# Turning between two sets of PSUM banks in an MLP's second product, and starting its first product early, in a two-layer hybrid network

## The chip, the cores and the metric

The kernel runs on one core of a Trainium2 chip. The metric is device time in microseconds (us) for one execution of the whole program, less is better. Names of engines: PE multiplies matrices (TensorE) and PEld is its loading of weights, DVE is VectorE, ACT is ScalarE, POOL is GpSimd, and SP issues the DMAs.

## The reference

A two-layer network on 1024 tokens with a model width of 1024, all in fp32. Layer 0 mixes tokens by attention in a sliding window, layer 1 by a gated recurrence (HGRN2), and each is followed by the same MLP, which is where the change lies:

```python
def sqrelu_mlp(h, w_up, w_down):
    return jnp.square(jax.nn.relu(h @ w_up)) @ w_down

for layer in range(DEPTH):                      # 2
    h = rmsnorm(x, mix_norm[layer])
    y = attention(h) if layer % 2 == 0 else hgrn2(h)
    x = x + y
    h = rmsnorm(x, mlp_norm[layer])
    x = x + sqrelu_mlp(h, w_up[layer], w_down[layer])   # w_up 1024x4096, w_down 4096x1024
return rmsnorm(x, final_norm)
```

## The kernel before, in words

**Precision.** Every fp32 operand is split into two numbers of a shorter format, a high part `hi` and the rest `lo`. A product is three matmuls (`mm3`): hi·hi, hi·lo, lo·hi. A split (`split`, `weight_split`) is one cast, on ACT or DVE, and one subtraction on DVE. Weights that are split as they come lie in small rings of buffers, `wr` (raw), `wh` and `wl` (5 of each); activations and everything that lives longer lie in the 60 buffers named `a`; `t` (18) and `m` (7) are for short use.

**Strassen.** Both products of the MLP are done by one level of Strassen's scheme (Winograd's form), with seven products, numbered 1 to 7, in place of eight. Sums of blocks of the weights and of the activations are made on DVE before, and sums of the results after.

**The first product** (`pair`, 16 calls with m = 0 to 15) makes rows m and m+16 of the hidden layer, each 128 wide, for both halves of the 512+512 tokens. Products 1 and 2 need the first half of the tokens only (`self.b[1]`, `self.b[2]`, made by `begin`), the others need sums with the second half (`finish`). Pairs 0 and 1 do all seven at full size (`leaves` empty); from pair 2 on, products 2 and 4 go one Strassen level deeper and are put together for two pairs at a time. The squared ReLU of each result is written to DRAM (`self.hid`).

**The second product** (`down`) has 16 steps p over the hidden layer, and the results of all steps are summed up in PSUM: four banks `main` (tag `q`) and four banks `side` (tag `p`), one bank for each 128 output columns of one half of the output. A step of one product is 12 matmuls of 512 columns, three into each of four banks. A *pass* (`run_pass`) does all 16 steps of one product, so 192 matmuls; operands are prepared up to two steps ahead (`operands`), by loads from DRAM, one or two sums, and two splits. Products 1, 6, 7 and 4 accumulate in `main`, which goes on from one to the next, and what stands in it after a product is copied out by ACT before the next product is added; products 5, 2 and 3 use `side`. The first pass does 1 and 5 step by step in turn. `T[p]` and `S[p]` are running sums of activations and of weights, kept from pass to pass in `a` buffers. Before, the passes are:

(1,5), 6, 7, 4, 2, 3

so that after (1,5) three passes in a row write `main`, and then two in a row write `side`. The last 4 steps of pass 3 (8 in layer 1) are held back and done at the end, bank by bank, under the beginning of what follows: in layer 0 the recurrence's normalisation and first products (`hgrn_first`, `hgrn`), in layer 1 the final norm (`final`).

**The order of the work.** The code only records operations. A planner (`Schedule.order`) then goes through time with a cost for each operation, gives buffers in the order of the program, and on each engine takes the operation with the lowest rank (its place in the program, less a lead for loads and splits of weights) among those that are ready. So each engine has a fixed list, worked off strictly in that order on the chip: an instruction that waits holds up all behind it. An operation with two possible engines (a cast) goes to where the planner sees it done first. All instructions carry line 334 in the profile, that of the call that issues them; so groups are told apart by names of buffers.

Of the kernel before, what the change touches and what calls it, by code (L numbers as in the profile page):

```python
# [14 lines left out]
ALU = mybir.AluOpType  # L15
# [3 lines left out]
T = 1024  # L19
# [3 lines left out]
TH = T // NH  # L23
# [112 lines left out]
LEAD = 100  # L136
WARM = 8
EVACUATE = 100
HK = KT // 2
# [140 lines left out]
class Net:  # L280
# [38 lines left out]
    def a(self, dt=F32, shape=(P, TH)):  # L319
        return self.tile("a", BUFS["a"], shape, dt)  # L320
# [251 lines left out]
        self.weigh(0)  # L572

    def mlp_second(self):
        x = self.finish(2 + self.layer, keep=True)
        self.weigh(1)
        return x
# [72 lines left out]
    def inner_products(self, leaf, w, x, sums, steps):  # L650
# [6 lines left out]
        for step in steps:  # L657
# [7 lines left out]
                self.tt("DVE", z, z, ps, ALU.add, 2 * P)  # L665
            yield

    def pair(self, m, x, leaves=()):

        up = self.io["up"][self.layer]
        first, second, half = up[m], up[m + MT // 2], MT // 2
        inner = []
        for leaf, now in leaves.items() if leaves else ():
            if now and leaf == 2:
                inner.append((2, up[m - 1][:, TH:], None))
            elif now:
                k = m - 1 if m == half - 1 else m - 2  # L680
                inner.append((4, up[k + half][:, TH:], up[k + 1 + half][:, TH:]))
        w = self.strassen_weights(first, second, tuple(leaves) if leaves else (), inner)

        def read(ps):
            z = self.t()
            self.copy(z, ps)
            return z

        parts = []

        def between():
            for z in parts:
                next(z, None)

        main, side = self.psum("q"), self.psum("q")
        self.product(main, w[1], x[1], True)
        u1 = read(main)
        if not leaves:
            own = self.psum()
            self.product(own, w[2], x[2], True)  # L700
            self.tt("DVE", u1, own, u1, ALU.add)
            self.square_relu(m, 0, u1, False)
        else:
            self.sums[2].append((m, u1))
            for leaf, now in leaves.items():
                if now and (leaf == 2 or m < half - 1):
                    sums = [z for _, z in self.sums[leaf][-2:]] if leaf == 2 else [z for _, z in self.sums[4][-2:]]
                    parts.append(self.inner_products(leaf, w, now, sums, ((1, 2), (6, 5), (7, 3), (4,))))
        between()
        self.product(side, w[5], x[5], True)  # L710
        p5 = read(side)
        between()
        self.product(main, w[6], x[6], False)
        u2 = read(main)
        self.product(side, w[3], x[3], False)
        between()
        self.tt("DVE", u2, side, u2, ALU.add)
        self.square_relu(m, 1, u2, False)
        last = leaves and leaves.get(4) and m == half - 1
        if last:  # L720
            u3 = self.t()
            z = self.inner_products(4, w, leaves[4], [self.sums[4][-1][1], u3], ((1, 2), (6,), (5, 7), (3, 4)))
            next(z)
        self.product(main, w[7], x[7], False)
        if last:
            next(z)
            self.copy(u3, main)
        else:
            u3 = read(main)
        between()  # L730
        self.tt("any", p5, p5, u3, ALU.add)
        self.square_relu(m + half, 1, p5, False)
        if not leaves:
            self.product(main, w[4], x[4], False)
            self.square_relu(m + half, 0, main, True)
            return
        if last:
            run(z)
            self.sums[4].append((m + half, u3))
            for n, u in self.sums[2][-2:] + self.sums[4][-2:]:  # L740
                self.square_relu(n, 0, u, False)
            return
        if leaves.get(2):
            for n, u in self.sums[2][-2:]:
                self.square_relu(n, 0, u, False)
        if leaves.get(4):
            for n, u in self.sums[4][-2:]:
                self.square_relu(n, 0, u, False)
        self.sums[4].append((m + half, u3))
# [26 lines left out]
    def operands(self, name, p, T, S, held=False):  # L776

        a = lambda i, k: self.raw(self.io["down"][self.layer, k, p, :, i])
        h = lambda i, hf: self.hidden(i, hf, p)

        def sum_of(tile, x, y, alu=ALU.subtract):
            self.tt("any", tile, x, y, alu)
            return tile

        if name == 1:
            self.corner = a(0, 0), h(0, 0)
            w, x = self.corner
        elif name == 5:
            first, q00 = self.corner
            T[p] = x = sum_of(self.a(), h(0, 1), q00)  # L790
            w = sum_of(self.t(tag="m"), a(1, 0), a(1, 1), ALU.add)
        elif name == 6:
            T[p] = x = sum_of(T[p], h(1, 1), T[p])
            w = S[p]
        elif name == 7:
            x = sum_of(self.t(), h(1, 1), h(0, 1))
            w = sum_of(self.t(tag="m"), a(0, 0), a(1, 0))
        elif name == 4:
            x = sum_of(T[p], h(1, 0), T[p])
            w = a(1, 1)  # L800
        elif name == 2:
            w, x = a(0, 1), h(1, 0)
        else:
            x = h(1, 1)
            w = sum_of(S[p], a(0, 1), S[p])
        got = self.split(w) if held else self.weight_split(w), self.split(x)
        if name == 5:
            S[p] = sum_of(self.a(), w, first)
        return got

    def down(self, cut):
# [4 lines left out]
        n, ahead = MT // 2, 2  # L816
# [4 lines left out]
        def products(names, ps, ws, start, stop, tokens=slice(0, TH), ms=range(HK)):  # L821
            for p in ps:
                for name in names:
                    (wh, wl), (xh, xl) = ws[name, p]
                    for m in ms:
                        out = (main if name in (1, 6, 7, 4) else side)[m][:, tokens]
                        c = slice(m * P, m * P + P)
                        more = {"skip_group_check": True} if name in (6, 7, 4) or not start else {}
                        first = p == 0 and not more
                        self.mm3(out, (wh[:, c], wl[:, c]), (xh[:, tokens], xl[:, tokens]), first, p == stop,  # L830
                                 tokens.stop - tokens.start, **more)

        def run_pass(names, held=0):
            ws, todo = {}, list(range(n))
            for p in range(n):
                while todo and todo[0] <= p + ahead or (todo and todo[0] >= n - held and p >= n - held - 1):
                    q = todo.pop(0)
                    for name in names:
                        ws[name, q] = self.operands(name, q, T, S, q >= n - held)
                if p < n - held:  # L840
                    products(names, [p], ws, True, n - held - 1)
            return ws

        def scaled_sum(hf, out, z, tokens=slice(0, TH)):
# [7 lines left out]
        def residual(m, hf):  # L852
            z = self.a()
            self.dma(z, self.x[m][hf], 4 * P * TH)
            return z

        run_pass((1, 5))
        for m in range(HK):
            y[0, 0, m], y[1, 1, m] = self.a(), self.a()
            self.copy(y[0, 0, m], main[m])  # L860
        for m in range(HK):
            self.copy(y[1, 1, m], side[m])
        run_pass((6,))
        for m in range(HK):
            u = y[0, 1, m] = self.a()
            self.copy(u, main[m])
        for m in range(HK):
            self.tt("DVE", y[0, 1, m], y[0, 1, m], y[1, 1, m], ALU.add)
        run_pass((7,))
# [5 lines left out]
        for i in range(2):  # L875
            for m in range(HK):
                z = residual(m + (1 - i) * HK, 1)
                scaled_sum(1, z, y[1 - i, 1, m])
                self.x[m + (1 - i) * HK][1] = z
        run_pass((4,))  # L880
        for m in range(HK):
            z = residual(m + HK, 0)
            scaled_sum(0, z, main[m])
            self.x[m + HK][0] = z
        run_pass((2,))
        parts = [self.t() for _ in range(HK)]
        for m in range(HK):
# [1 line left out]
        for m in range(HK):  # L889
            self.tt("DVE", y[0, 0, m], parts[m], y[0, 0, m], ALU.add)  # L890
            z = residual(m, 0)
            scaled_sum(0, z, y[0, 0, m])
            self.x[m][0] = z
        if not cut:
            held = 4
            ws = run_pass((3,), held)
            yield 0, slice(0, TH)
            for m in range(HK):
                products((3,), range(n - held, n), ws, False, n - 1, ms=[m])
                scaled_sum(1, self.x[m][1], side[m])  # L900
            yield 1, slice(0, TH)
            return
        held = n // 2
# [637 lines left out]
```

## Time and profile before

| | |
|---|---|
| three runs | 2151.45, 2154.43, 2158.83 us |
| the profiled execution | 2151.11 us, of which the profile's span is 2149.3 us |
| granted PE clock, mean | 0.996 |
| DVE busy | 1866.9 us (87%) |
| ACT busy | 993.3 us (46%) |
| moved by DMA | 333.91 MB, 155 GB/s on average |
| layer 0: first products / second products | 344 to 636 us / 636 to 938 us |
| layer 1: first products / second products | 1504 to 1817 us / 1817 to 2110 us |

Times within the execution count from the start of the span. In the rows of the profile, a group such as `q<-a,wh` is an instruction that writes a `q` bank from an `a` buffer and a `wh` buffer. `[2.30 <-ACT t]` at the end of a row of the timeline is the idle time of the engine before it, and the engine and buffer that ended it. A matmul's row is longer than its share of PE, since matmuls overlap; the distance of two starts tells the pace. Rows by stretch give, for each engine, busy time and the number of instructions, then the granted PE clock (1.00 is full), the share of the DMA engines, and GB/s.

### The profile page before, as it was taken

Reading aid. Unit: us, or ns where it says so; the run is one execution under the profiler, and the core shown is the slowest. Engines: PE = TensorE matmul, PEld = TensorE weight load, DVE = VectorE, ACT = ScalarE, POOL = GpSimd, SP = SyncE. Lnnn points to the kernel's source line nnn. Section 1 sums busy time; section 2 is a strip of 40 time slices with the busy share of each in tenths; the row PEclk is TensorE's granted clock in tenths of the full one; section 3 lists DMA queues with packets and bytes.
Section 4 is the critical chain, followed back from the end, with each engine's and each line's share of the span. In section 5 each row is a group of like instructions: output and inputs, shape, how many; then the busy total and the mean of one; then the engine's idle time right before and its main releaser. Section 6 shows DMA issues by size and latency. Waiting matters only on the chain.

```text
span 2149.3 us, 33980 instructions
## 1 busy us (share of the span) xinstructions
PE 2114.5 (98%) x11968; PEld 1734.0 (81%) x11968; DVE 1866.9 (87%) x3822; ACT 993.3 (46%) x2031; POOL 61.7 (3%) x121
## 2 busy tenths in 40 slices
PE   9999999999999999999999999999999999999998
PEld 7778777888888887877788888788788888888787
DVE  8889899888899988899888888878988889899886
ACT  5567777444454234465333333343644445423444
POOL 4020000000000000000100000000000000000000
PEclk9999999999999999999999999999999999999999
DMA  6212275443468876731111111547444446897652
GB/s 214 77 50 83 80 245 167 131 134 124 137 197 293 299 248 219 255 111 55 59 60 55 60 55 60 189 155 227 165 133 133 128 132 202 282 301 244 200 177 79
DMA packets 183787, 333.91 MB, mean 155 GB/s; under 512 B 20672, under 2 KB 22720, under 8 KB 183616
## 3 DMA queue, kind: packets, MB, share of 16 engines
q1 hardware_dynamic: 183616, 331.74, 47.3%
q8 instruction: 94, 1.54, 0.3%
q14 instruction: 77, 0.63, 0.1%
HBM read 265.60 MB, written 66.06 MB: 154 GB/s over the span
## 4 chain that ended last, share of the span: by engine, by line
PE 54%; issue 36%; DVE 5%; ACT 3%; DMA 1%; SPq 0%; POOL 0%; POOLq 0%; ACTq 0%; DVEq 0%
PE p L334 29%; PE q L334 25%; DVE a L334 2%; DVE t L334 2%; ACT a L334 1%; ACT t L334 1%; DVE wl L334 1%; DVE m L334 1%; DMA t<-d 0%; ACT wh L334 0%; DVE wh L334 0%; DMA wr<-in_up 0%; DVE sm L334 0%; DMA a<-in_x 0%; DMA d<-t 0%
## 5 line engine op out<-in xcount | busy, mean ns | idle before, releaser
L334 PE MATMUL p<-a,wh 128*128 128x512 f32 (+1 forms) x2616 | 775.0, 378 | 5.8 <-ACT wh L334 4.0
L334 PE MATMUL q<-a,wh 128*128 128x512 f32 x2336 | 734.9, 396 | 6.8 <-ACT t L334 5.0
L334 PEld LDWEIGHTS p<-a,wh 128*128 128x128 f32 x2616 | 469.3, 188 | 96.5 <-ACT wh L334 5.0
L334 PEld LDWEIGHTS q<-a,wh 128*128 128x128 f32 x2336 | 432.1, 189 | 102.6 <-ACT t L334 7.5
L334 PE MATMUL p<-a,wl 128*128 128x512 f32 (+1 forms) x1308 | 488.5, 374 | 1.8 <-DVE wl L334 1.7
L334 PE MATMUL q<-a,wl 128*128 128x512 f32 x1168 | 460.9, 395 | 0.3 <-DVE wl L334 0.3
L334 PEld LDWEIGHTS p<-a,wl 128*128 128x128 f32 x1308 | 246.3, 188 | 46.9 <-DVE wl L334 2.7
L334 PEld LDWEIGHTS q<-a,wl 128*128 128x128 f32 x1168 | 220.1, 188 | 52.7 <-DVE wl L334 0.8
L334 DVE TENSOR_TENSOR wl<-wr,wh 128x512 fp32r<-128x512 f32 x352 | 241.2, 687 | 15.6 <-ACT wh L334 5.3
L334 ACT ACTIVATE t<-t 128x512 f32<-128x512 f32 x238 | 148.1, 631 | 169.8 <-DVE t L334 163.5
L334 DVE TENSOR_TENSOR wl<-m,wh 128x512 fp32r<-128x512 f32 x312 | 212.5, 687 | 5.1 <-ACT wh L334 0.4
L334 DVE TENSOR_TENSOR a<-t,a 128x512 fp32r<-128x512 f32 (+2 forms) x304 | 199.1, 677 | 3.4 <-DMA t<-d 2.9
L334 ACT COPY t<-q 128x512 f32<-128x512 f32 (+2 forms) x201 | 111.1, 559 | 193.0 <-PE q L334 171.7
L334 ACT CAST a<-t 128x512 fp32r<-128x512 f32 (+1 forms) x203 | 121.5, 611 | 144.1 <-PE q L334 73.9
L334 ACT CAST wh<-wr 128x512 fp32r<-128x512 f32 x180 | 111.1, 620 | 162.8 <-PE p L334 93.0
L334 DVE TENSOR_TENSOR t<-t,t 128x512 f32<-128x512 f32 (+3 forms) x299 | 173.6, 599 | 12.2 <-DMA t<-d 6.2
L334 ACT CAST wh<-m 128x512 fp32r<-128x512 f32 x200 | 123.5, 622 | 128.6 <-PE p L334 66.1
L334 DVE CAST wh<-wr 128x512 fp32r<-128x512 f32 x172 | 73.5, 428 | 118.2 <-PE q L334 78.5
L334 DVE TENSOR_TENSOR m<-wr,wr 128x512 f32<-128x512 f32 (+1 forms) x188 | 119.3, 647 | 18.8 <-DMA wr<-in_down 16.1
L334 PE MATMUL p<-wh,a 128*128 128x512 f32 x384 | 126.0, 399 | 0.5 <-ACT a L334 0.4
L334 PEld LDWEIGHTS q<-t,t 128*64 128x64 f32 (+1 forms) x2160 | 98.0, 144 | 25.0 <-issue 10.9
L334 PE MATMUL q<-t,t 128*64 128x32 f32 (+2 forms) x2160 | 111.5, 230 | 0.0
(125 smaller groups left out, 2323.7 us busy)
## 6 DMA issues: line engine op xcount, KB each, us to landing
t<-d SPq DMA_DIRECT2D x312, 256.0 KB, 4.7
wr<-in_down SPq DMA_DIRECT2D x256, 256.0 KB, 4.1
d<-t SPq DMA_DIRECT2D x188, 256.0 KB, 3.1
wr<-in_up SPq DMA_DIRECT2D x170, 256.0 KB, 3.1
wr<-in_win SPq DMA_DIRECT2D x68, 256.0 KB, 2.8
a<-d SPq DMA_DIRECT2D x60, 256.0 KB, 4.4
wr<-in_wqkv SPq DMA_DIRECT2D x48, 256.0 KB, 2.9
d<-a SPq DMA_DIRECT2D x48, 256.0 KB, 3.4
```

Of the source, the lines that this page charges most:

```text
L334: fn(*[place(a) for a in args], **{k: place(v) for k, v in kw.items()})
```

## The change

Two things are done, in both layers.

**Passes in turn.** The passes become (1,5), 6, 7, 2, 4, 3. The last step of product 5 (p = 15) is taken out of the first pass (`kept`): its operands are split into `a` buffers, and its 12 matmuls into `side` stand after pass 6. `side` is copied out after that and no more after (1,5). With 2 ahead of 4, pass 2 makes the weight sum of pass 3, `S[p] = a01 - S[p]`, from the block that it has loaded for itself, and pass 3 loads and sums no weights any more (16 loads less in each layer). `T[p]`, which pass 4 uses last, lives through pass 2.

**Products 1 and 2 of pairs 0 and 1 first.** A new function `pair_first` is called for m = 0 and 1 at the start of `mlp_second`, ahead of `finish`: it loads and splits the two blocks of weights, does products 1 and 2 on the first half of the tokens, adds them and writes the squared ReLU; the `q` bank with product 1 is handed on to `pair`, which goes on with 5. `pair` still loads the two blocks for its sums of weights, so each block comes twice (4 more loads in each layer).

In all, the list of SP has 24 rows less; the numbers of matmuls, of sums and of splits stay the same.

```diff
     def mlp_second(self):
+        self.first = [self.pair_first(m) for m in range(2)]
         x = self.finish(2 + self.layer, keep=True)
...
+    def pair_first(self, m):
+        self.s.lead = LEAD
+        up = self.io["up"][self.layer, m]
+        w = [self.weight_split(self.raw(up[:, c : c + TH])) for c in (0, TH)]
+        self.s.lead = 0
+        main, own, u1 = self.psum("q"), self.psum(), self.t()
+        self.product(main, w[0], self.b[1], True)
+        self.copy(u1, main)
+        self.product(own, w[1], self.b[2], True)
+        self.tt("DVE", u1, own, u1, ALU.add)
+        self.square_relu(m, 0, u1, False)
+        return main
...
-        w = self.strassen_weights(first, second, tuple(leaves) if leaves else (), inner)
+        w = self.strassen_weights(first, second, tuple(leaves) if leaves else (1, 2), inner)
...
-        main, side = self.psum("q"), self.psum("q")
-        self.product(main, w[1], x[1], True)
-        u1 = read(main)
-        if not leaves:
-            own = self.psum()
-            self.product(own, w[2], x[2], True)
-            self.tt("DVE", u1, own, u1, ALU.add)
-            self.square_relu(m, 0, u1, False)
-        else:
+        main, side = self.psum("q") if leaves else self.first[m], self.psum("q")
+        if leaves:
+            self.product(main, w[1], x[1], True)
+            u1 = read(main)
...
         elif name == 2:
             w, x = a(0, 1), h(1, 0)
+            S[p] = sum_of(S[p], w, S[p])
         else:
-            x = h(1, 1)
-            w = sum_of(S[p], a(0, 1), S[p])
+            w, x = S[p], h(1, 1)
...
-        def run_pass(names, held=0):
+        def run_pass(names, held=0, kept=()):
...
-                        ws[name, q] = self.operands(name, q, T, S, q >= n - held)
+                        ws[name, q] = self.operands(name, q, T, S, q >= n - held or (name, q) in kept)
                 if p < n - held:
-                    products(names, [p], ws, True, n - held - 1)
+                    products([name for name in names if (name, p) not in kept], [p], ws, True, n - held - 1)
...
-        run_pass((1, 5))
+        ws = run_pass((1, 5), kept=[(5, n - 1)])
         for m in range(HK):
-            y[0, 0, m], y[1, 1, m] = self.a(), self.a()
+            y[0, 0, m] = self.a()
             self.copy(y[0, 0, m], main[m])
-        for m in range(HK):
-            self.copy(y[1, 1, m], side[m])
         run_pass((6,))
+        products((5,), [n - 1], ws, True, n - 1)
...
+        for m in range(HK):
+            y[1, 1, m] = self.a()
+            self.copy(y[1, 1, m], side[m])
...
-        run_pass((4,))
-        for m in range(HK):
-            z = residual(m + HK, 0)
-            scaled_sum(0, z, main[m])
-            self.x[m + HK][0] = z
         run_pass((2,))
...
+        run_pass((4,))
+        for m in range(HK):
+            z = residual(m + HK, 0)
+            scaled_sum(0, z, main[m])
+            self.x[m + HK][0] = z
```

Three places of the engines' lists are shown, each before and after. The numbers behind a buffer's name tell one use of it from another.

First, PE in layer 0 at the end of pass 7, before. The banks `q1694` to `q1697` are `main`:

```order
L334 MATMUL q1697_7375<-a2208_9057,wh2206_9106 128x512
L334 MATMUL q1697_7375<-a2209_9067,wh2206_9106 128x512
L334 MATMUL q1697_7375<-a2208_9057,wl2207_9112 128x512
L334 MATMUL q1694_7326<-a2234_9136,wh2232_9132 128x512
L334 MATMUL q1694_7326<-a2235_9177,wh2232_9132 128x512
L334 MATMUL q1694_7326<-a2234_9136,wl2233_9139 128x512
```

and the same place after, where `q1698` to `q1701` are `main` and `p1702` to `p1705` are `side`:

```order
L334 MATMUL q1701_7383<-a2212_9036,wh2210_9083 128x512
L334 MATMUL q1701_7383<-a2213_9044,wh2210_9083 128x512
L334 MATMUL q1701_7383<-a2212_9036,wl2211_9089 128x512
L334 MATMUL p1702_7392<-a2238_9113,wh2236_9107 128x512
L334 MATMUL p1702_7392<-a2239_9142,wh2236_9107 128x512
L334 MATMUL p1702_7392<-a2238_9113,wl2237_9120 128x512
```

Behind pass 7 stood pass 4, in the same four banks; now pass 2 stands there, in the other four.

Second, ACT in layer 1 after the end of the recurrence's output product, before. `q3846` holds product 1 of pair 0, `q3847` its product 5, `wh3866` is the weight of pair 1's product 1; `a3793` to `a3801` are operands of product 4 that `finish` makes:

```order
L334 CAST wh3866_16618<-wr3858_16392 128x512
L334 CAST a3793_16623<-t3792_16484 128x512
L334 CAST a3797_16629<-t3796_16494 128x512
L334 CAST a3801_16635<-t3800_16505 128x512
L334 CAST wh3844_16641<-wr3827_16358 128x512
L334 COPY t3848_16645<-q3846_16521 128x512
L334 COPY t3851_16647<-q3847_16582 128x512
```

and after, where `q3738` and `q3748` hold product 1 of pairs 0 and 1:

```order
L334 ACTIVATE t3777_16520<-a3731_16511,c01_91 128x512
L334 COPY t3740_16529<-q3738_16492 128x512
L334 ACTIVATE t3812_16535<-a3661_16123 128x512
L334 ACTIVATE t3813_16542<-a3671_16169 128x512
L334 CAST a3778_16547<-t3777_16520 128x512
L334 CAST wh3842_16555<-m3837_16504 128x512
```

The copy of product 1 stood behind the casts of the operands of product 4 and now stands ahead of them, among the first instructions after the last row of `x`.

Third, ACT in layer 0 in pass 3, before. `wh2480` is the weight of step 6, `wh2486` to `wh2504` those of steps 7 to 10; the rows with `t` on the left or right belong to the recurrence's beginning:

```order
L334 CAST wh2492_10309<-a1845_7746 128x512
L334 CAST a2555_10313<-t2554_10028 128x512
L334 CAST a2559_10319<-t2558_10050 128x512
L334 CAST a2563_10326<-t2562_10071 128x512
L334 ACTIVATE t2576_10332<-a2330_9421 128x512
L334 CAST wh2486_10338<-a1829_7696 128x512
L334 CAST wh2498_10342<-a1861_7797 128x512
L334 CAST wh2504_10346<-a1877_7862 128x512
L334 CAST a2567_10348<-t2566_10107 128x512
L334 ACTIVATE t2577_10352<-a2332_9431 128x512
L334 CAST wh2480_10356<-a1813_7631 128x512
```

and after, where `wh2477` is the weight of step 6, `wh2482` that of step 7 and `wh2487` that of step 8:

```order
L334 CAST wh2482_10272<-a1833_7704 128x512
L334 ACTIVATE t2565_10276<-a2444_9884 128x512
L334 CAST a2543_10283<-t2542_10173 128x512
L334 CAST wh2477_10289<-a1817_7639 128x512
L334 CAST a2547_10295<-t2546_10182 128x512
L334 CAST wh2487_10301<-a1849_7754 128x512
```

The weight of step 6 stood behind those of the four steps that follow it, and now stands behind that of step 7 alone.

## The prediction

> **What bounds the kernel now.** I read the page's first part, then who waited for whom on PE, then the stretches around those waits in the timeline.
>
> ```profile
> span 2149.3 us, 33980 instructions
> PE 2114.5 (98%) x11968; PEld 1734.0 (81%) x11968; DVE 1866.9 (87%) x3822; ACT 993.3 (46%) x2031; POOL 61.7 (3%) x121
> PE q L334 <- ACT t L334: 6.9, 6, 2.3
> PE p L334 <- ACT wh L334: 4.0, 1, 4.0
> PE q L334 <- ACT wh L334: 1.7, 2, 1.5
> ```
>
> PE is busy for 98% of the span, and the change takes no matmul away. So what can be won is only where PE waits, or runs slowly: the last three rows say that it waited 6.9 us, in 6 waits, for results of ACT in `t`, once 4.0 us for a weight in `wh`, and 1.7 us for other such weights.
>
> ```profile
> 725.40:769.90 44.50, 44.50 (x193) 35.93 (x193) 40.01 (x72) 11.37 (x20) 0.00 (x0) 1.00 0.69 226
> 926.23:929.64 3.41, 3.41 (x9) 2.76 (x9) 3.41 (x11) 2.25 (x4) 0.00 (x0) 0.50 0.00 0
> 1516.73:1520.14 3.41, 3.41 (x8) 2.74 (x9) 3.41 (x6) 2.59 (x5) 0.00 (x0) 0.50 0.23 79
> 1998.01:2001.42 3.41, 3.41 (x8) 2.73 (x9) 3.41 (x7) 3.06 (x6) 0.00 (x0) 0.50 0.61 174
> ```
>
> The first row is pass 6 of layer 0, undisturbed: 192 matmuls in 44.5 us at clock 1.00, 0.232 us each. The other three are stretches at half the clock: 8 or 9 matmuls in 3.41 us, where 8 take 1.86 us and 9 take 2.09 us, so 1.55, 1.55 and 1.32 us lost in each. Each begins where a wait of PE ends, so a wait there costs itself and the half clock behind it.
>
> **The change part by part.** *Pass 7 to the next pass.* In layer 1, PE and ACT at the end of pass 7, and what DVE waited for in pass 7; the last row is PE's wait at the same place in layer 0:
>
> ```profile
> 1995.31 0.40 PE L334 MATMUL q<-a,wl 128*128 128x512 f32 x1
> 1996.85 0.62 ACT L334 CAST a<-a 128x512 fp32r<-128x512 f32 x1 [0.86 <-DVE a L334]
> 1997.38 1.55 ACT L334 COPY t<-q 128x512 f32<-128x512 f32 x3
> 1998.01 1.22 PE L334 MATMUL q<-a,wh 128*128 128x512 f32 x2 [2.30 <-ACT t L334]
> ...
> DVE a L334 <- DMA a<-d: 1.6, 2, 1.4
> ...
> PE q L334 <- ACT t L334: 0.8, 1, 0.8
> ```
>
> PE has done pass 7 at 1995.3 and needs `main` copied out before pass 4 writes it. ACT comes to these copies at 1997.4 only, since the cast ahead of them in its list waits for DVE, and DVE had waited 1.6 us for rows of `x` that come back from DRAM. With pass 2 behind pass 7, PE writes `side`, and the same late copies are wanted 44.5 us later. Gain: 2.30 + 1.55 = 3.85 us in layer 1, 0.82 us in layer 0. What could be late in its place is an operand of pass 2: in the new lists the steps of pass 2 after the first four have their last operand at least 6 DVE instructions ahead of PE's turn. At 0.60 us each (five sums start 1506.98 to 1509.99, below) that is 3.6 us, over the 1.6 us; cost 0.
>
> *The beginning of layer 1's MLP.* PE, ACT and DVE:
>
> ```profile
> 1503.93 0.39 PE L334 MATMUL p<-a,wl 128*128 128x512 f32 x1
> 1512.26 0.40 PE L334 MATMUL q<-a,wl 128*128 128x512 f32 x1
> 1514.12 0.72 PE L334 MATMUL q<-a,wh 128*128 128x512 f32 x2 [1.47 <-ACT wh L334]
> 1516.68 1.21 PE L334 MATMUL q<-a,wh 128*128 128x512 f32 x2 [1.84 <-ACT t L334]
> 1516.05 1.06 ACT L334 COPY t<-q 128x512 f32<-128x512 f32 x2
> 1506.98 3.09 DVE L334 TENSOR_TENSOR t<-t,t 128x512 f32<-128x512 f32 x5
> 1509.99 3.09 DVE L334 TENSOR_TENSOR a<-t,a 128x512 fp32r<-128x512 f32 x5
> ```
>
> The recurrence's output product ends on PE at 1503.9, and then products 1, 2 and 5 of pair 0 are all there is: 36 matmuls, 8.35 us, up to 1512.3. Then PE waits for the next pair's weight (1.47 us), and product 6 waits 1.84 us for the copy of product 1 out of its bank, which stood behind the casts of product 4's operands on ACT. Lost: 1.47 + 1.84 + 1.55 = 4.86 us. Now 60 matmuls stand there (products 1 and 2 of both pairs, then 5), 13.9 us, and the copy is early. Product 6's last operand is the 15th DVE instruction from the read of the output product's last bank on: 15 x 0.60 = 9.0 us and about 1 us until DVE starts, so some 10 us against 13.9. The added work: 4 loads of 256 KB, in a stretch with DMA to spare (the row 1516.73 has a share of 0.23), and pair 1's splits, copy, addition and squared ReLU, which only come earlier. DVE does them within those 15; what they push back are the operands of products 7 and 4, needed 19 and 22 us after 1503.9. I take 0.5 us as left, between 0 (the room of 3.9 us holds) and the 1.84 us of the wait that was there. In layer 0 there is no such row of any size between 344 and 367 us; I take 0.
>
> *Pass 3 and the recurrence's beginning, layer 0.*
>
> ```profile
> 919.00:925.20 6.20, 2.24 (x10) 1.50 (x8) 6.20 (x11) 6.20 (x12) 0.13 (x1) 1.00 0.15 42
> 924.61 0.60 ACT L334 CAST wh<-a 128x512 fp32r<-128x512 f32 x1
> 925.26 0.96 PE L334 MATMUL p<-a,wh 128*128 128x512 f32 x3 [4.02 <-ACT wh L334]
> ...
> 769.90:815.00 45.10, 44.53 (x193) 35.78 (x191) 41.59 (x72) 15.77 (x29) 0.00 (x0) 1.00 0.86 290
> 815.00:860.00 45.00, 44.76 (x193) 36.27 (x194) 36.71 (x63) 17.75 (x32) 0.00 (x0) 1.00 0.67 208
> 860.00:904.60 44.60, 44.60 (x194) 36.13 (x193) 35.86 (x63) 16.05 (x28) 0.00 (x0) 1.00 0.78 250
> 904.60:938.00 33.40, 29.38 (x120) 23.42 (x119) 33.40 (x83) 26.42 (x49) 0.36 (x2) 0.95 0.45 151
> ```
>
> Here nobody waits but PE: DVE and ACT are busy for all of 919.0 to 925.2 (6.20 of 6.20), and DVE for all of 904.6 to 938.0. PE waits 4.02 us for step 6's weight, cast last of its neighbours, and runs at half clock after it: 4.02 + 1.32 = 5.34 us. The change takes 16 weight sums out of pass 3 (9.6 us of DVE at 0.60), and four additions from what precedes it: pass 2's results were copied and added before scaling, pass 4's are scaled straight from PSUM. So DVE has up to 12 us less here, over the 5.34, and the new list has step 6's weight split 5 matmul groups of three before PE's turn. The sums go into pass 2. Its DVE work is then what pass 4 had (a sum and two subtractions a step, and the 20 instructions that finish passes 5 and 7): the 36.7 us of row 815 against 44.6 us of PE. Pass 4, without those 20 but with 8 scalings and 4 additions of pass 2's results, comes to 36.71 - 8 x 0.60 = 31.9 us. Both are below row 769.9's 41.59, under which PE ran without a wait until its end. I take 0.5 us of the 5.34 as left, between 0 and the whole.
>
> *The edge from (1,5) to 6.* Before, product 5's last step (12 matmuls, 2.8 us) lay between the last write of `main` by 1 and the first by 6. Now 6 follows at once. Layer 1, where DMA is nearest to its limit:
>
> ```profile
> 1817.00:1906.00 89.00, 88.61 (x388) 71.76 (x387) 80.06 (x136) 39.83 (x71) 0.00 (x0) 1.00 0.88 288
> ...
> DVE m L334 <- DMA wr<-in_down: 8.2, 9, 1.9
> ...
> 1900.92 0.62 ACT L334 CAST a<-a 128x512 fp32r<-128x512 f32 x1 [2.16 <-PE p L334]
> 1901.86 1.97 ACT L334 COPY a<-q 128x512 f32<-128x512 f32 x3 [0.31 <-PE q L334]
> 1905.37 0.69 DVE L334 TENSOR_TENSOR wl<-a,wh 128x512 fp32r<-128x512 f32 x1
> 1906.51 0.63 PE L334 MATMUL q<-a,wh 128*128 128x512 f32 x2
> 1906.98 0.39 PE L334 MATMUL q<-a,wl 128*128 128x512 f32 x1
> ```
>
> The copies start 0.3 us after PE has written the first bank, and ACT is idle before them, so the first bank is free at about 1902.5, 1.2 us ahead of its next use even without 5 between (1906.5 - 2.8 = 1903.7). The operands are nearer: DVE waited 8.2 us for weights in this pass, and pass 6's first low part ends at 1906.06, 0.92 us before its matmul at 1906.98. In the new lists pass 6's operands move up by as many DVE instructions as PE comes earlier, less one, so 0.92 - 0.60 = 0.3 us is left. I take 0.5 us lost in layer 1 for it. Bounds: a gain is excluded, since PE does not wait there now; above, DVE may be late by the whole 2.8 us, then half clock: 4.35 us. It is nearest to the lower end, by the 0.3. After pass 6, product 5's step covers the copies of `main`; there was no wait to take away.
>
> *Sum.* 3.85 + 0.82 + 4.86 + 5.34 = 14.87 us, less 0.5 + 0.5 + 0.5, is 13.4 us. The profiled execution took 2151.11 us and would take 2137.7. The median of the runs, 2154.43, is 3.3 us higher; I leave that distance and predict 2141 us.
>
> **The rivals.** *The edge fails.* Pass 6 finds its operands 2.8 us late, at half clock after: 4.35 us in place of the 0.5 in layer 1, and in layer 0 too if DMA waits are as long there. Gain 9.5 or 5.2 us, 2145 to 2149 us. For it: the reserve of 0.3 us. Against: DVE's list moves with PE's.
>
> *DVE only moves the wait.* Sums moved into pass 2 make its operands late, or pass 3 keeps its wait. It gives back the 5.34: 2146 us. For it: DVE busy all of 904.6 to 938. Against: rows 815 and 860, with 8 us of DVE idle in each.
>
> *Slower.* The first pass's DMA waits on DVE (8.2 us in 9 waits) come through to PE once the 2.8 us at its end no longer fill DVE's backlog. From the point where the reserve is below zero, each wait is PE's: 8.2 us, and six half clocks of 1.4 us, 16.6 us a layer. In both layers: 2141 + 33 = 2174 us; in one it would be about no change or a little slower (2157). Against: under those waits PE was busy for 88.61 of the 89.00 us of this pass (its row stands ahead of the waits).
>
> *Half clocks are not of the waits.* Two of the three follow waits of 2.30 us and of 1.47 + 1.84 us. The Trainium skill (TensorE: Matmul & The Clock Gate, section "Why this matters for your kernels") says the clock drops after PE idles for more than about 3 us. If these two stay when the waits go, the gain is 13.4 - 3.1 = 10.3 us, 2144 us. The rows speak against this rule: a half clock begins within 0.1 us of the end of both waits.
>
> *Turning between banks costs clock.* Passes on two sets of banks in turn could make PE idle for a moment at each change; with a half clock of 1.55 us at four more changes in each layer, 12.4 us, the time would be 2153 us. The same page of the Trainium skill ("A second HAM failure mode: psum-queue depth-cycling") reports a kernel that lost its clock by cycling through banks. Against: (1,5) turns between the sets at every step already, and the rows 1901 to 1907 show full pace.
>
> **How the numbers follow.** Chances: forecast 0.70; edge 0.11; DVE 0.08; slower 0.04; clock not of the waits 0.05; banks 0.02. 0.3% (6.5 us) is about what a measurement of this kernel can tell from no change, so faster is below 2148: the forecast, DVE, the clock and two thirds of the edge, 0.88 with some taken off for what is unknown. Around no change: the rest of the edge, banks, part of slower, 0.08; slower 0.04. The range: below, nothing left or lost (14.87) from the profiled 2151.1, and some 3 us more where the runs' own spread (2151.45 to 2158.83) held such waits: 2133. Above, the edge in both layers, 2149, with 2 us of spread: 2151.
>
> **What would show it.** Right: no wait of PE for `t` behind pass 7, in either layer; none over 1 us in 1500 to 1525 or in pass 3 of layer 0; no half clock between the first matmuls and the end but a short one; DVE less than full in pass 3. Wrong: PE waiting for `wl` at the start of pass 6, or a new wait in pass 2.

## The result, and the profile after

The changed kernel took 2134.97 us (median of 6 runs, 2134.27 to 2137.78) against 2153.54 us before (6 runs, 2148.07 to 2158.83). The ratio is 0.9919, 95% interval 0.9907 to 0.9931, which is 17.4 us less (14.9 to 20.0); the medians differ by 18.6 us. Gains against the kernel before are worked out from ratios in this way below. The forecast was 2141 us and a gain of 13.4 us, in a range of 2133 to 2151. The profiled execution took 2136.34 us.

From the page's first part and from who waited for whom on PE, after:

```profile
span 2134.6 us, 33918 instructions
PE 2108.3 (99%) x11968; PEld 1732.8 (81%) x11968; DVE 1866.6 (87%) x3828; ACT 992.3 (46%) x2026; POOL 59.8 (3%) x121
PE q L334 <- ACT t L334: 3.0, 4, 1.3
PE q L334 <- ACT wh L334: 0.2, 1, 0.2
```

PE's waits for `t` fell from 6.9 to 3.0 us, those of `q` for `wh` from 1.7 to 0.2, and the row for `p` and `wh` (4.0 us) is gone. DVE's and ACT's busy times are the same within 1 us: the work did not shrink, PE only waits less. By stretch (columns as before: busy time and instructions of PE, PEld, DVE, ACT, POOL, then the clock), after:

```profile
815.50:817.50 2.00, 2.00 (x10) 1.64 (x9) 2.00 (x4) 1.89 (x5) 0.00 (x0) 1.00 0.25 61
905.11:938.00 32.89, 32.89 (x144) 26.69 (x143) 29.97 (x77) 19.87 (x36) 0.00 (x0) 1.00 0.45 153
1501.00:1525.00 24.00, 22.99 (x101) 18.09 (x99) 24.00 (x41) 18.45 (x34) 0.00 (x0) 1.00 0.67 217
1982.00:1986.00 4.00, 4.00 (x19) 3.26 (x18) 3.23 (x7) 3.34 (x7) 0.00 (x0) 1.00 0.53 173
```

The first and last row hold the edges from pass 7 to pass 2 (816.2 and 1984.95 us): PE is busy throughout. The second is pass 3 of layer 0: 144 matmuls in 32.9 us, where 120 took 33.4 before. The third is the beginning of layer 1's MLP, the only one of the four places with a wait left, and the clock is 1.00 in all four. What is left there, in the timeline of PE and then of ACT, after:

```profile
1520.26 0.40 PE L334 MATMUL q<-a,wl 128*128 128x512 f32 x1
1520.63 0.73 PE L334 MATMUL q<-a,wh 128*128 128x512 f32 x2
1522.37 0.74 PE L334 MATMUL q<-a,wh 128*128 128x512 f32 x2 [1.01 <-ACT t L334]
...
1521.22 0.62 ACT L334 CAST wh<-m 128x512 fp32r<-128x512 f32 x1 [0.64 <-DVE m L334]
1521.74 0.58 ACT L334 COPY t<-q 128x512 f32<-128x512 f32 x1
```

This is product 4 of pair 0, which waits for the copy of product 7 out of its bank: three matmuls begin in 2.11 us, where 0.70 would do. The copy stands behind a cast that had waited 0.64 us for DVE.

Where the time went, summed over the starts of all matmuls of PE: the distance of two starts beyond the usual one of that kind of matmul (0.232 us for 512 columns) is time lost.

| place | lost before, us | lost after, us |
|---|---|---|
| start of the program (to 45 us) | 4.4 | 7.2 |
| layer 0: turn from first to second products | 1.6 | 1.4 |
| layer 0: behind pass 7 | 1.1 | 0 |
| layer 0: pass 3 | 5.8 | 0 |
| layer 0: between pass 3 and the recurrence's loop | 2.3 | 1.8 |
| layer 1: beginning of the MLP | 5.4 | 1.5 |
| layer 1: turn from first to second products | 1.7 | 1.2 |
| layer 1: behind pass 7 | 4.1 | 0 |

Without the first row that is 16.1 us less, with it 13.3 us; the two spans differ by 14.7 us, and the rest is spread over many small places. The first row is not the change's: it lies ahead of every changed instruction, and in the twelve other profiles below this stretch lost between 4.8 and 6.6 us, whichever the kernel.

### The profile page after: what moved, and what is told of

The parts are those of the page before. It is cut to its first block, busy times and chain, and to the rows that moved or that the text cites. A ratio compares the mean times of both kernels' runs of the same rounds, so it can differ in the third digit from the quotient of the medians.

```text
span 2134.6 us, 33918 instructions
## 1 busy us (share of the span) xinstructions
PE 2108.3 (99%) x11968; PEld 1732.8 (81%) x11968; DVE 1866.6 (87%) x3828; ACT 992.3 (46%) x2026; POOL 59.8 (3%) x121
## 4 chain that ended last, share of the span: by engine, by line
PE 86%; DVE 8%; issue 2%; DMA 2%; ACT 1%; POOL 0%; SPq 0%; POOLq 0%; DVEq 0%; ACTq 0%
PE q L334 44%; PE p L334 41%; DVE t L334 3%; DVE a L334 2%; DVE wl L334 1%; DVE m L334 1%; ACT a L334 1%; DMA wr<-in_up 0%; DVE wh L334 0%; DMA t<-d 0%; DMA wr<-in_win 0%; DMA a<-in_x 0%; ACT t L334 0%; DVE sm L334 0%; DMA c<-in_par 0%
## 5 line engine op out<-in xcount | busy, mean ns | idle before, releaser
L334 ACT CAST wh<-wr 128x512 fp32r<-128x512 f32 x191 | 117.8, 619 | 162.6 <-PE p L334 96.2
L334 DVE TENSOR_TENSOR t<-t,t 128x512 f32<-128x512 f32 (+4 forms) x299 | 173.4, 598 | 12.3 <-DMA t<-d 7.3
L334 ACT CAST wh<-m 128x512 fp32r<-128x512 f32 x187 | 115.4, 622 | 115.7 <-PE p L334 61.2
L334 DVE CAST wh<-wr 128x512 fp32r<-128x512 f32 x161 | 68.8, 427 | 100.2 <-PE q L334 70.6
L334 DVE TENSOR_TENSOR m<-wr,wr 128x512 f32<-128x512 f32 (+1 forms) x188 | 119.3, 645 | 17.4 <-DMA wr<-in_down 14.4
```

Source lines behind the costliest of these rows:

```text
L334: fn(*[place(a) for a in args], **{k: place(v) for k, v in kw.items()})
```

## The experiments

Each kernel ran in five rounds beside the kernel before on the same chip; ratios are to before, with their intervals. The kernels of the first group shared one chip, those of the second (rows_later, early_half, act_only, four_later) another, the last four a third. Before took 2150.39, 2149.89 and 2148.51 us there.

**The two halves apart.** `order_only` is the changed kernel without `pair_first`, `first_only` the kernel before with it.

```diff
 order_only, against after
-        self.first = [self.pair_first(m) for m in range(2)]
 first_only, against before
+        self.first = [self.pair_first(m) for m in range(2)]
```

> The new order of the passes with the last step of product 5 behind pass 6 and the weight sums in pass 2, but products 1 and 2 of pairs 0 and 1 as before. Theory A (each part took away the waits that stood at its own place, and they add up): the wait for `t` behind pass 7 and the wait for a weight in pass 3 of layer 0 are gone, the two waits at the beginning of layer 1's MLP (1.5 and 1.8 us) and the half clock behind them are back: about 12 to 14 us faster than before, ratio 0.994. Theory B (the early products matter beyond their place, since they shift the lists of all engines behind them): other waits come back too, less than 8 us faster.

> Products 1 and 2 of pairs 0 and 1 early, the passes as before. Theory A: only the beginning of the MLP changes, 4 to 5 us faster (two waits of 1.5 and 1.8 us and 1.5 us by half clock go, a wait of 1.0 us behind product 7 comes), ratio 0.998; behind pass 7 of layer 1 PE waits 1.5 to 2.5 us for `t` with half clock after it, and 4 us for a weight in pass 3 of layer 0. Theory B: more than 8 us faster.

`order_only` took 2139.09 us, ratio 0.9952 (0.9940 to 0.9964), 10.3 us less; `first_only` 2145.00 us, 0.9974 (0.9960 to 0.9988), 5.6 us less. Together 0.74%, against 0.73% (after_again, below) and 0.81% of both: the halves add up, as theory A has it, though `order_only` falls short of the 12 to 14 us that were expected. In `order_only`'s profile the two waits at the beginning of layer 1's MLP are back (1.44 and 1.83 us, with a half clock behind them), and there is none behind pass 7 nor in pass 3. In `first_only`'s those are there, in the timeline of PE:

```profile
818.68 0.74 PE L334 MATMUL q<-a,wh 128*128 128x512 f32 x2 [1.80 <-ACT t L334]
929.72 1.22 PE L334 MATMUL p<-a,wh 128*128 128x512 f32 x2 [3.44 <-ACT wh L334]
1997.37 0.92 PE L334 MATMUL q<-a,wh 128*128 128x512 f32 x2 [2.87 <-ACT t L334]
```

**Which part of the order.** `swap_only` exchanges passes 4 and 2 and nothing else; `sums_only` moves the weight sums and nothing else.

```diff
 swap_only, against before: the lines from run_pass((4,)) to self.x[m + HK][0] = z
 stand behind those of run_pass((2,))
 sums_only, against before
         elif name == 2:
             w, x = a(0, 1), h(1, 0)
+            S[p] = sum_of(S[p], w, S[p])
         else:
-            x = h(1, 1)
-            w = sum_of(S[p], a(0, 1), S[p])
+            w, x = S[p], h(1, 1)
```

> From the kernel before, only passes 4 and 2 change places; the weight sums stay in pass 3, with their loads, and product 5 stays whole in the first pass. Theory A, as predicted (pass 3's wait comes of the 16 weight sums that DVE does there): the wait behind pass 7 goes in both layers (0.8 + 3.9 us), the wait of about 4 us for a weight in pass 3 of layer 0 stays with its half clock: about 5 us faster. Theory C (pass 3's wait comes of what stands ahead of it, four copies on ACT and four additions on DVE of pass 2's results that the list must place in pass 3's first steps; behind pass 4 there are none): pass 3's wait goes too, about 10 to 11 us faster. In the new list step 6's weight no longer stands right ahead of PE's turn, which speaks for C.

> From the kernel before, only the weight sums S = a01 - S move from pass 3 into pass 2 (16 loads and 16 sums less in pass 3, no load more in pass 2); order of the passes as before. Theory A (DVE's load in pass 3): pass 3's wait of 4.0 us and its half clock go, 5 us faster; the wait behind pass 7 of layer 1 stays at 1.5 to 2.5 us. Theory C (what stands ahead of pass 3): its wait stays at 2 to 4 us and the time within 2 us of before.

`swap_only` took 2140.09 us, 0.9954 (0.9942 to 0.9966), as much as the whole of `order_only`. `sums_only` took 2151.06 us, 1.0005 (0.9995 to 1.0014): no change. Pass 3 of layer 0 by stretch, in `swap_only` and then in `sums_only`, with PE's wait there in the latter:

```profile
905.98:939.00 33.02, 33.02 (x144) 26.85 (x143) 31.77 (x80) 22.48 (x40) 0.36 (x2) 1.00 0.51 172
```

```profile
909.50:942.00 32.50, 30.11 (x124) 23.99 (x123) 31.36 (x80) 26.11 (x48) 0.36 (x2) 0.95 0.35 121
928.45 0.90 PE L334 MATMUL p<-a,wh 128*128 128x512 f32 x2 [2.39 <-ACT wh L334]
```

So the 16 weight sums in pass 3, on which the prediction built its second largest term, are not what made its wait. One row could have told it: DVE's groups in the kernel before, from the beginning of pass 3 to the end of the wait (904.6 to 926 us), have the weight sums as `a<-wr,a`:

```profile
L334 DVE TENSOR_TENSOR a<-wr,a 128x512 f32<-128x512 f32 x2 | 1.4, 681 | 0.0
```

Two of the sums stood there, 1.4 us. The others had been done ahead.

**What makes pass 3 wait.** Two explanations were left: the work that pass 2's results bring into pass 3 (theory C), or the place of one cast in ACT's list (theory P). `early_half` takes the work away, `act_only` changes the list at the same work.

```diff
 early_half, against before
+        for m in range(HK):
+            z = residual(m, 0)
+            scaled_sum(0, z, y[0, 0, m])
+            self.x[m][0] = z
         run_pass((2,))
-        parts = [self.t() for _ in range(HK)]
...
+        for m in range(HK):
+            scaled_sum(0, self.x[m][0], side[m])
 act_only, against before
-    def weight_split(self, z):
+    def weight_split(self, z, engines=("ACT", "DVE")):
...
-        got = self.split(w) if held else self.weight_split(w), self.split(x)
+        got = self.split(w) if held else self.weight_split(w, ("ACT",) if name == 3 else ("ACT", "DVE")), self.split(x)
```

> From the kernel before, the half of `y[0, 0]` that is known before pass 2 is scaled and added to `x` ahead of pass 2, so that behind pass 2 its banks are scaled straight from PSUM, as pass 4's are: no copies on ACT, no four additions on DVE behind pass 2, eight instructions of DVE more ahead of it. Theory C (work that pass 2's results bring into the first steps of pass 3 makes its weight late): the wait for a weight in pass 3 of layer 0 (4.0, 3.4 and 2.4 us in the three profiles with pass 2 ahead of pass 3) goes, 4 to 5 us faster. Theory P (the wait is where the order of the lists puts one step's cast behind those of the steps after it, which in this list is the weight of step 5 in place of step 6): a wait of over 1.5 us stays, one step earlier, and the time is within 3 us of before.

> From the kernel before, the casts of pass 3's weights that are split as they come may go on ACT alone, not on DVE. Work and order of the passes are those of before, but in ACT's list these casts now stand in the order of their steps, each 12 or more ACT instructions ahead of PE's turn. Theory P: the wait for a weight in pass 3 of layer 0 goes with its half clock, 4 to 5.5 us faster; the wait behind pass 7 stays. Theory C: with the same work the wait stays, at another step or of another buffer, and the time is that of before.

`early_half` took 2149.00 us, 0.9996 (0.9984 to 1.0007). The wait stayed, one step earlier, where its list has the cast of step 5 last:

```profile
921.98 1.19 PE L334 MATMUL p<-a,wh 128*128 128x512 f32 x4 [1.85 <-ACT wh L334]
```

`act_only` has no wait in pass 3, with the work and the order of passes of before: in both traces all 17 casts into `wh` between 890 and 945 us are on ACT and none on DVE, and their order is what the edit changes. Theory P holds: the wait is where the planner's list puts one step's cast behind those of the steps after it. But the 4 to 5.5 us that were expected did not come: 2147.82 us, 0.9992 (0.9981 to 1.0002). They were given back 45 us later, at the recurrence's first products:

```profile
970.30 0.74 PE L334 MATMUL p<-a,wh 128*128 128x512 f32 x2 [2.75 <-ACT wh L334]
```

With its half clock this place lost 5.5 us, against the 1.4 us of before. The weight that PE waits for there is cast from a sum of DVE, and DVE has next to no room between the two places (`act_only`):

```profile
928.00:970.00 42.00, 39.55 (x179) 32.02 (x177) 40.56 (x99) 26.15 (x47) 0.00 (x0) 1.00 0.34 113
```

It is busy for 40.56 of the 42.00 us, which fits a list that serves pass 3 earlier and something behind it later; this step was not tried by itself. Nor was why the exchange of passes escapes it. `swap_only`'s list puts pass 3's casts in the order of their steps, like `act_only`'s, and its profile loses 1.3 us at the second place; over the same 42 us DVE is busy for 39.24 us in it and for 36.59 us in the changed kernel.

**What makes the copies behind pass 7 late.** `rows_later` leaves the order of the passes and moves the residual sums that come between.

```diff
 rows_later, against before: these lines, from behind run_pass((7,)) to behind run_pass((4,))
         for i in range(2):
             for m in range(HK):
                 z = residual(m + (1 - i) * HK, 1)
                 scaled_sum(1, z, y[1 - i, 1, m])
                 self.x[m + (1 - i) * HK][1] = z
```

> From the kernel before, the eight residual sums that follow pass 7 (their rows of `x` come back from DRAM, and DVE waits for them in pass 7) are written behind pass 4. Nothing is left out; the order of the passes is that of before. Theory A, as predicted (the late rows hold up DVE, so a cast on ACT, so the copies of `main` behind it): the wait for `t` behind pass 7, 0.8 to 2.5 us in layer 0 and 1.5 to 2.9 us in layer 1 by the four profiles in which pass 4 follows pass 7, falls below 0.5 us in both layers, and no half clock stands there: 3 to 6 us faster. Rival (four banks that are written again at once always cost a wait, whatever DVE does): both waits stay within the spans named.

It took 2145.51 us, 0.9978 (0.9968 to 0.9987), 4.7 us less. PE has no wait behind pass 7 in either layer, with pass 4 behind it in the same four banks; the stretches with these edges in `rows_later` (layers 0 and 1), and ACT's copies in layer 1:

```profile
813.00:818.00 5.00, 5.00 (x23) 4.08 (x22) 4.96 (x11) 4.09 (x8) 0.00 (x0) 1.00 0.32 104
1990.00:1996.00 6.00, 6.00 (x27) 4.89 (x26) 5.96 (x13) 5.01 (x9) 0.00 (x0) 1.00 0.37 117
...
1990.91 1.98 ACT L334 COPY t<-q 128x512 f32<-128x512 f32 x3
```

Three copies in 1.98 us keep pace with PE, which finishes a bank every 0.70 us; in the kernel before they came at once, three in 1.55 us, behind a late cast. Theory A holds, the rival falls: four banks written again at once cost nothing if the copies start in time. The same can be read in the changed kernel, where PE goes on in the other banks, at the edge in layer 1:

```profile
1983.07 1.97 ACT L334 COPY t<-q 128x512 f32<-128x512 f32 x3 [0.31 <-PE q L334]
1984.95 0.62 PE L334 MATMUL p<-a,wh 128*128 128x512 f32 x2
```

The first bank was copied by 1983.65 (a copy takes 0.58 us in this trace), 1.3 us before pass 2 began. By these rows the turn to the other banks was not needed there. What helped was not tried by itself. Pass 2's operands, plain rows of the hidden layer, need no sum on DVE behind which a cast of ACT could be late: ACT's last cast ahead of the copies waited for PE (1.64 us), where before it had waited for DVE (0.86 us). DVE's own waits for the rows of `x` were shorter too, 0.5 us against 1.6.

**The other parts of the change.** `swap_first` is the changed kernel without the kept step and without the moved sums; `no_kept` is without the kept step alone; `after_again` is the changed kernel, on the same chip.

```diff
 no_kept, against after
-        ws = run_pass((1, 5), kept=[(5, n - 1)])
+        run_pass((1, 5))
...
         run_pass((6,))
-        products((5,), [n - 1], ws, True, n - 1)
```

> The changed kernel unchanged, beside the next three on one chip, as their measure: 2133 to 2137 us, ratio to before 0.992 to 0.993.

> The changed kernel without two of its parts: product 5 stays whole in the first pass (its banks copied out there), and the weight sums stay in pass 3 with their 16 loads a layer. What is left is the exchange of passes 2 and 4 and the early products of pairs 0 and 1. Theory P (pass order and list decide, the moved step and the moved sums do nothing): the changed kernel's time within 2 us, no wait behind pass 7 and none in pass 3 of layer 0. Theory A, as predicted (16 weight sums out of pass 3 matter): a wait in pass 3 of layer 0 of 1 to 4 us comes back, 3 to 5 us slower than the changed kernel.

> The changed kernel with product 5's last step back in the first pass, so that 12 matmuls stand between the last write of `main` by 1 and the first by 6, and none between 6 and 7. As predicted the kept step costs 0.5 us in layer 1 at the edge to pass 6 and saves nothing behind pass 6: 0 to 1 us faster than the changed kernel. Rival (the kept step covers the copies of `main` behind pass 6): a wait of PE for `t` or `a` between passes 6 and 7, 1 to 3 us slower.

`after_again` took 2133.70 us, 0.9927 (0.9914 to 0.9940); `no_kept` 2134.91 us, 0.9935 (0.9922 to 0.9948); `swap_first` 2135.89 us, 0.9938 (0.9925 to 0.9951). The intervals overlap. Neither profile has a wait between passes 6 and 7, behind pass 7 or in pass 3 of layer 0, so neither rival is seen. `swap_first`'s 2.2 us over `after_again` are a little more than the 2 us that were allowed; its profile has a wait of 1.87 us at 376 us, in the first products of layer 0, where the changed kernel's two profiles have none and 0.44 us and `order_only`, which has the kept step and the moved sums, has 1.67 us. That these two parts earn a microsecond or two is thus not shown, nor excluded.

**Two attempts at what is left.** Both start from the changed kernel and aim at the wait of 1.0 us at the beginning of layer 1's MLP.

```diff
 four_later: product 4 of pair 0 behind product 5 of pair 1
         p5 = read(side)
+        if m == 1:
+            self.rest()
 evacuate_q: copies out of q banks ranked like those out of p banks
-        if any(isinstance(v, View) and v.buf.tag == "p" for v in ins):
+        if any(isinstance(v, View) and v.buf.tag in ("p", "q") for v in ins):
             lead = max(lead, EVACUATE)
```

> From the changed kernel, product 4 of pair 0 comes behind product 5 of pair 1, so that 12 matmuls (2.8 us) lie between product 7 and product 4, which share a bank. If the wait of 1.0 us there is for the copy of product 7 alone, it goes: about 1.2 us faster than the changed kernel in layer 1, 0 to 1 us in layer 0, ratio to before 0.991. If DVE, busy without a break there, is what is late, another wait of about a microsecond takes its place and the time is the changed kernel's.

> The changed kernel with one condition of the planner's ranks widened: reads of `q` banks get the lead of 100 places that reads of `p` banks have, so that copies out of `q` stand ahead of casts in ACT's list. In the changed kernel's profile PE waits 3.0 us in 4 waits for copies into `t` out of `q`, 1.0 us of it at the beginning of layer 1's MLP. If these waits come of the place of the copies in ACT's list, 1 to 3 us faster than the changed kernel; if the casts that are pushed back are needed as soon, the same time or up to 3 us slower.

`four_later` took 2134.51 us, 0.9922 (0.9908 to 0.9935). In layer 1 the planner put PE's list in the same order at this place as without the edit, and the wait is there (0.93 us), so it tests nothing there. `evacuate_q` took 2132.65 us, 0.9924 (0.9911 to 0.9938). In its profile PE does not wait at the beginning of layer 1's MLP, so with the copies further ahead in ACT's list the wait goes; that all lists changed with it keeps this from being a test of the one place. 1.05 us under `after_again` is less than the intervals can tell, so it is not shown to be the faster kernel.

## Why the prediction was right, point by point

- *Behind pass 7* (3.85 + 0.82 us): right in size (4.1 + 1.1 us by the table) and in the cause, the residual sums with their late rows of `x` (`rows_later`). The remedy was described wrongly: "the same late copies are wanted 44.5 us later" never came about, since with pass 2 behind them the copies are no longer late.
- *The beginning of layer 1's MLP* (4.86 us, 0.5 left): the waits went. "What they push back are the operands of products 7 and 4" named the place of the new wait, product 4, but what is late there is the copy of product 7 out of its bank, not an operand. 1.5 us were lost by the table, not 0.5.
- *Pass 3* (5.34 us, 0.5 left): 5.8 us came, for a reason that was not the one given, so that this term came out right is luck. The step "the change takes 16 weight sums out of pass 3 (9.6 us of DVE at 0.60)" failed: only 2 were there, and moving them alone did nothing (`sums_only`). The quoted sign of the true cause, that step 6's weight is "cast last of its neighbours", stood in the same paragraph as a remark. DVE's load was mis-sized as well. It was to have up to 12 us less in pass 3 and is busy for 29.97 us there, 3.4 less than before; passes 2 and 4 were put at 36.7 and 31.9 us, and DVE is busy for 44.08 of 44.50 us (816.0 to 860.5) and 40.90 of 44.60 us (860.0 to 904.6). PE waited in neither pass, so a full DVE alone made nothing late.
- *The edge from (1,5) to 6* (0.5 us lost in layer 1): nothing was lost; no wait over 0.3 us stands at either edge. In the changed kernel's layer 1, DVE and PE there:

```profile
1892.57 0.69 DVE L334 TENSOR_TENSOR wl<-a,wh 128x512 fp32r<-128x512 f32 x1
1893.22 0.63 PE L334 MATMUL q<-a,wh 128*128 128x512 f32 x2
1893.68 0.39 PE L334 MATMUL q<-a,wl 128*128 128x512 f32 x1
```

  The low part ends at 1893.26, 0.42 us before its matmul, close to the 0.3 us that were worked out; the 0.5 us put on top were caution.
- *Sum and base*: the terms gave 13.4 us, and the same four places gave 14.9 us by the table, which counts a wait from start to start; two places that the sum did not have, the turn from the first to the second products and the recurrence's beginning, gave 1.2 us more. The two profiled executions differ by 14.8 us. The step that was most off is "I leave that distance" between the profiled execution before and the median, 3.3 us: the profiled execution after lies 1.4 us above its median, the one before 2.4 us below that of its six runs, and these 3.8 us are the rest of the 18.6. On the third chip the medians of the same two kernels differ by 14.8 us (2148.51 and 2133.70), so the gain of 17.4 us may be on the high side. What made the distance was not measured. Waits at the places of the change are of other lengths in each profile: in the five with pass 4 behind pass 7 and the residual sums between them 0.8, 1.2, 1.3, 1.8 and 2.5 us in layer 0 and 0.7, 1.1, 1.5, 2.3 and 2.9 us in layer 1, and in pass 3, in the four with step 6's weight last, 2.4, 3.4, 3.4 and 4.0 us. But these are five kernels with one profile each, not runs of one kernel. The runs show that the spread went: 21 of before in the first chip's job lie between 2146.80 and 2160.42 us, the 11 of the changed kernel in all jobs between 2132.74 and 2137.78 us.
- *Rivals*: none came. The edge kept its reserve; the 8 us of idle DVE that were to speak against late operands in pass 2 were not there (0.4 us), and still none was late; DVE's 8.2 us of waits for weights (5.6 us after) stayed hidden; the turns between banks cost no clock, PE being at 1.00 at all of them; the half clocks went with the waits, except that a half clock is not the price of every wait (below).

## What to carry to other kernels

When PE waits at a change of banks, look at the copying engine first: copies that follow PE's pace say that the banks are free in time, copies in a burst say that something ahead of them in that engine's list was late, and moving that something may do as much as more banks. Before a wait is put down to the amount of work, see whether the awaited instruction stands behind those of later steps in its list; where a planner sets the lists, an edit that frees one place can fill another, so the gain is read some tens of microseconds further on as well. And a kernel is to be compared at the median of its runs: here the two profiled executions lay 2.4 us below and 1.4 us above theirs.

## What the runs showed of the hardware

The half clock has a grid. In every profile the starts of the half clocks lie whole multiples of 3.413 us apart (before: 926.23, 1516.73 and 1998.01 are 173.0 and 141.0 of them apart), not where a wait ends, as the prediction has it: the first began 0.97 us after the wait in pass 3 was over. What decides, as far as these traces show, is how busy PE was in the stretch of the grid just ended. In `first_only` a wait of 1.80 us inside one stretch was enough; the rows are the stretch with the wait and the next:

```profile
816.75:820.16 3.41, 1.60 (x7) 1.24 (x7) 3.36 (x7) 2.63 (x6) 0.00 (x0) 1.00 0.45 150
820.16:823.57 3.41, 3.41 (x9) 2.65 (x8) 3.41 (x7) 2.58 (x5) 0.00 (x0) 0.50 0.58 185
```

In `rows_later` the wait for pass 3's weight took 3.38 us, but lay across the border of two stretches, and no half clock followed:

```profile
920.28:923.69 3.41, 1.59 (x7) 0.95 (x6) 3.41 (x7) 3.41 (x8) 0.00 (x0) 1.00 0.01 4
923.69:927.11 3.42, 1.86 (x8) 1.50 (x9) 3.42 (x6) 1.51 (x3) 0.00 (x0) 1.00 0.00 0
927.11:930.52 3.41, 3.41 (x17) 2.78 (x16) 3.41 (x13) 3.14 (x6) 0.00 (x0) 1.00 0.00 0
```

Over the 14 profiles, between 10 and 2110 us, 15 stretches had PE busy for under 0.50 of the time by the trace's modelled ends, and all but one (the first row here, 0.47) were followed by a half clock; of those with 0.50 to 0.70 one was (0.51). One half clock does not fit: at 2109.25 us in `act_only` it follows a stretch with PE busy for 0.94, in which 16 of the 27 matmuls have a single column; why is open. So the border is near one half, and the same wait costs the 1.3 to 1.6 us of a half clock more or not, by where it falls. The Trainium skill (TensorE: Matmul & The Clock Gate, section "What's actually happening") has the window of 3413 ns that runs freely, and the trace agrees. The section "Why this matters for your kernels" of the same page of the Trainium skill, by which the clock drops after more than about 3 us of idling, does not fit: 1.80 us were enough, and 3.38 us were not.
